# Measured charges and a shared read port in the clock that orders a two-network kernel

## The chip, the cores and the metric

The kernel runs on one core of a Trainium2 chip. The metric is the device time of one execution in microseconds (us). The core's engines are TensorE (PE in the rows; PEld are its weight loads), VectorE (DVE), ScalarE (ACT), GpSimd (POOL), and SyncE (SP), which issues most of the transfers. TensorE's clock has two levels here, 2.4 and 1.2 GHz; the profile gives the granted share of 2.4 GHz for any stretch.

## What is computed

Two networks run one after the other on 512 tokens of width 1024, in float32, and share nothing but the kernel. Cut to what matters:

```
# first network, one layer
h = h + 0.5 * rms_norm(swiglu(rms_norm(h), w_gate, w_up, w_down))
u = rms_norm(h) @ w_in                       # q, k, v of two mixers
o_a = stick_breaking_attention(...)          # 8 heads of 64
o_b = chunk_band_attention(...)              # 8 heads of 64, 9 chunks of 64
h = h + rms_norm(concat(rms_norm(o_a), rms_norm(o_b)) @ w_out)
h = h + 0.5 * rms_norm(swiglu(rms_norm(h), ...))
h = h + rms_norm((p @ w_proj) * sigmoid(h @ w_ple_gate))

# second network, four layers, x = x + mixer(rms_norm(x)), then a last norm
conv:  (b * causal_conv(c * v)) * silu(z) @ w_out
fox:   softmax(q k^T + forget decay) v, 8 heads of 128
gdn:   gated delta net, 8 heads of 128, chunks of 64: a triangular solve for each chunk
swa:   rotary, windowed attention of 128 with sinks, 16 heads of 64
```

## The kernel before

Activations stand transposed: a tile holds 128 channels by 512 tokens, and the residual stream is eight such tiles, h0 to h7. Weights come from HBM as 128x512 chunks into four staging tiles (`wst`), and each chunk is split in two: ScalarE copies the high part (fp32r), VectorE subtracts it for the low part. A product is three fp32r matmuls (high by high, low by high, high by low), summed in a PSUM bank.

An rms norm needs three steps that leave TensorE and come back. Squares of the eight h tiles are added into one tile (ScalarE squares, VectorE or GpSimd adds); TensorE sums the columns with matmuls of one column (`stats`, line 820, in the rows `ps<-cst,t ... 128x1`); a chain of small operations takes the reciprocal root, on VectorE with `soon`, else on GpSimd (`rsqrt`, line 786, thirteen operations); and TensorE spreads it over the rows by transposes (`rows`, line 842, in the rows `ps<-cst,b 128x128` of line 687). Only then can results be scaled. So that TensorE does not stand still, matmuls of the next weights are put between these steps: each layer's first products run on the unscaled h.

Nothing here is ordered by hand. The program is written out instruction by instruction, and a clock kept while that is done (lines 255 to 590) decides what comes next. `free[...]` holds for each engine the time at which it comes free, each tile the time of its last write or read. Calls on VectorE, ScalarE, GpSimd and SyncE go through `Eng` (line 358), which charges them by formulas and leaves them pending as `Op`; `next_op` (line 336) takes the one that can start first (among those within 20 ns the one of the best rank) and `trace` writes it out. TensorE's matmuls are charged by `mm` (line 669) and `transpose` (line 684) and written out at once by `product`. Side tasks are generators (the norms, the heads of the mixers); between the matmuls of a weight product `poll` (line 566) runs a step of a side task when the clock says that what it needs is there. A charge that is changed therefore moves instructions on every engine, and each engine then works its list strictly in order.

Every recorded VectorE, ScalarE and GpSimd operation has line 391 in the rows, every matmul line 682 and every transpose line 687, since helpers write them out.

Of the kernel before, what the change touches and what calls it, by code (L numbers as in the profile page):

```python
# [201 lines left out]
def chain_kernel(ctx, tc, xT, pT, wall, params, consts, chbias, pos, out):  # L202
# [82 lines left out]
    table = [None]  # L285

    class Op:


        def __init__(self, key, run, outs, ins, cost, prio=0, func=None, more=0):  # L290
            self.key, self.run, self.outs, self.ins, self.cost, self.more = key, run, outs, ins, cost, more
            self.prio, self.func = prio, func
            self.deps, self.next = set(), []
            for x, w in [(x, True) for x in outs] + [(x, False) for x in ins]:
                for o in conflicts(x, w):
                    if o not in self.deps:
                        self.deps.add(o)
                        o.next.append(self)
            for x, w in [(x, True) for x in outs] + [(x, False) for x in ins]:
                live.setdefault(name(x), []).append((self, parts(x)[0], w))  # L300
            pending[key].append(self)
# [9 lines left out]

        def start(self):
            return max([free[self.key]] + [there(x, self.key) for x in self.ins] + [unused(x, self.key) for x in self.outs])

        def trace(self):
# [7 lines left out]
            self.run()  # L323
            free[self.key] = t
            pending[self.key].remove(self)
            for x in self.outs + self.ins:
# [9 lines left out]
    def next_op():  # L336

        best, when = None, NEVER
        for ops in pending.values():
            can = [(o.start(), o) for o in ops if not o.deps]  # L340
            if can:
                t0 = min(c[0] for c in can)
                t, o = min((c for c in can if c[0] <= t0 + 20), key=lambda c: c[1].rank())
                if t < when:
                    best, when = o, t
        return best, when

# [10 lines left out]
    class Eng:  # L358
# [6 lines left out]
        def __getattr__(self, op):  # L365
            f = getattr(self.eng, op)

            def call(*a, **kw):
# [19 lines left out]
                else:  # L388
                    a0, a1 = (258, 3.34) if ptr else self.POOL.get(op, (147, 2.1))
                    cost = a0 + a1 * n  # L390
                Op(self.key, lambda: f(*a, **kw), outs, ins, cost, self.prio, func, more)  # L391

# [265 lines left out]
    def product(ps, ins, ns):  # L658
# [8 lines left out]
        touch(ps, t + ns, "PE", True)  # L667

    def mm(ps, lhsT, rhs, start=True, stop=True, tile=None, **kw):
        ps, lhsT, rhs = raw(ps), raw(lhsT), raw(rhs)  # L670
        n = max(parts(rhs)[1], 64)
        if tile is not None:
            ns = tile
        elif rhs.dtype == F32:
            ns = 4 * n / 2.4 + 2.5
        elif rhs.dtype == F32R:
            ns = (n if n >= 256 else 4 * n) / 2.4 + 2.5
        else:
            ns = n / 2.4
        thin[0] = max(0.0, thin[0] + (ns if tile is not None else -0.5 * ns))  # L680
# [3 lines left out]
    def transpose(ps, src, idn):  # L684
        ps, src, idn = raw(ps), raw(src), raw(idn)
        product(ps, (src, idn), 107.0)
        PE.transpose(ps, src, idn)  # L687
# [110 lines left out]
    class Norm:  # L798
# [21 lines left out]
        def stats(self, cols, soon=False):  # L820
# [3 lines left out]
            for j in range(c0 // P, c1 // P):  # L824
                mm(pc[:, j : j + 1], self.acc[:, j * P : j * P + P], meanc[:, self.mcol : self.mcol + 1], start=j == c0 // P,
                   skip_group_check=True, tile=187)
            self.left -= c1 - c0
# [272 lines left out]
    def soft_heads(heads, span, done, own, causal=False, ready=lambda: True):  # L1100
# [46 lines left out]
        def weigh(qt):  # L1147
            k0, n = span(qt)
            for j in range(n // P):
                for i, (rows, qk, bias, values, sinks) in enumerate(heads):  # L1150
                    mm(po[rows, qt * P : qt * P + P], values(k0 // P + j), ptb[qt, i][:, j * P : j * P + P],
                       start=j == 0, stop=j == n // P - 1, skip_group_check=True, tile=134 if len(heads) > 1 else None)
            for i in range(len(heads)):
# [23 lines left out]
    def mixing(S1):  # L1177
# [45 lines left out]
        def sb_pair(p):  # L1223
# [93 lines left out]
            for kt in range(4):  # L1317
                for e in range(2):
                    hd = 2 * p + e
                    mm(po[rows[e], kt * P :], va[kt][:, hd * 64 : hd * 64 + 64], at_(a[place[kt, e][0]], kt, e), start=kt == 0, stop=kt == 3, skip_group_check=True,  # L1320
                       tile=0.95 * (S - kt * P))
            a.clear()
# [284 lines left out]
    def gdn_layer(S1):  # L1607
# [18 lines left out]
        def gates(t):  # L1626
            yield t[0:64]
            pt = PS("bat")
            for c in range(4):
                mm(pt[:, c * 16 : c * 16 + 16], t[0:64, c * P : c * P + P], con("ident32")[0:64, 0:16], tile=187)  # L1630
            del t
# [59 lines left out]
        def head(hd):  # L1691
# [88 lines left out]
            def mm32(ps, lhsT, rhs):  # L1780
                for c in range(4):
                    for g in range(4):
                        gs, cs = slice(32 * g, 32 * g + 32), slice(32 * c, 32 * c + 32)
                        mm(ps[gs, cs], lhsT[gs, cs], rhs[gs, cs], tile=34)

# [26 lines left out]
            for c in range(4):  # L1812
                cs = slice(32 * c, 32 * c + 32)
                for a, b in zip(lo, hi):
                    mm(p5[b, cs], nL[a, c * P + b.start : c * P + b.stop], Tm[a, cs], tile=34)
            for i, b in enumerate(hi):
# [7 lines left out]
            for c in range(4):  # L1824
                cs = slice(32 * c, 32 * c + 32)
                mm(p7[hi[0], cs], U[hi[0], cs], M5[hi[0], cs], tile=34)
                for a, b in zip(lo, hi):
                    mm(p6[a, cs], M5[b, cs], U[b, cs], tile=34)
            V.tensor_copy(blocks(T64[:, 0:256])[hi[0], :, 0:32], blocks(p7[:, 0:P])[hi[0]])
# [5 lines left out]
            for c in range(4):  # L1835
                cs = slice(64 * c, 64 * c + 64)
                mm(p8[64:P, cs], nL[0:64, c * P + 64 : c * P + P], T64[0:64, cs], tile=50)
            M6 = T64
# [301 lines left out]
```

## Time and profile before

| | |
|---|---|
| median of three runs | 2174.5 us (2173.39 to 2176.55) |
| profiled execution | 2176.79 us |
| its span, first to last instruction | 2175.1 us |
| mean granted TensorE clock | 0.990 |
| TensorE busy | 2116.3 us, 97% |
| VectorE busy | 1324.4 us, 61% |
| ScalarE busy | 999.2 us, 46% |
| GpSimd busy | 299.5 us, 14% |

The span is what the profile's rows cover; the 1.7 us between it and the execution's time lie outside of any instruction. A timeline row gives the start, the duration from the first to the last instruction of the row, engine, line, operation, output and inputs by the program's names, shape and count; in brackets stands the idle time of the engine ahead of the row and what ended it. A matmul's duration contains its way through the array, so the pace is read from a row of many.

### The profile page before, as it was taken

Reading aid. Unit: us, or ns where it says so; the run is one execution under the profiler, and the core shown is the slowest. Engines: PE = TensorE matmul, PEld = TensorE weight load, DVE = VectorE, ACT = ScalarE, POOL = GpSimd, SP = SyncE. Lnnn points to the kernel's source line nnn. Section 1 sums busy time; section 2 is a strip of 40 time slices with the busy share of each in tenths; the row PEclk is TensorE's granted clock in tenths of the full one; section 3 lists DMA queues with packets and bytes.
Section 4 is the critical chain, followed back from the end, with each engine's and each line's share of the span. In section 5 each row is a group of like instructions: output and inputs, shape, how many; then the busy total and the mean of one; then the engine's idle time right before and its main releaser. Section 6 shows DMA issues by size and latency. Waiting matters only on the chain.

```text
span 2175.1 us, 35809 instructions
## 1 busy us (share of the span) xinstructions
PE 2116.3 (97%) x13583; PEld 1778.1 (82%) x13583; DVE 1324.4 (61%) x2783; ACT 999.2 (46%) x2187; POOL 299.5 (14%) x600
## 2 busy tenths in 40 slices
PE   8999999999999999999999999999998999999998
PEld 7888889988779888889988887888877877778777
DVE  5433455787867442455785554266568677665896
ACT  5332333676855332333642234344446554533764
POOL 0000001311113000000120012000015242221320
PEclk9999999999999999999999999999999999999999
DMA  5232241222221332232223333312222222222221
GB/s 170 97 97 93 96 139 56 69 70 81 64 88 52 105 112 83 97 115 71 92 73 97 97 97 115 116 59 68 69 85 70 60 55 59 61 83 86 85 83 59
DMA packets 105404, 186.11 MB, mean 86 GB/s; under 512 B 12392, under 2 KB 18952, under 8 KB 105232
## 3 DMA queue, kind: packets, MB, share of 16 engines
q1 hardware_dynamic: 103920, 179.62, 26.6%
q0 software_dynamic: 1312, 4.21, 0.6%
q8 instruction: 106, 1.74, 0.3%
q14 instruction: 66, 0.54, 0.1%
HBM read 179.03 MB, written 2.13 MB: 83 GB/s over the span
## 4 chain that ended last, share of the span: by engine, by line
PE 82%; DVE 11%; POOL 3%; ACT 2%; issue 2%; DMA 1%; SPq 0%; DVEq 0%; POOLq 0%; ACTq 0%
PE ps L682 80%; DVE t L391 9%; ACT t L391 2%; PE ps L687 2%; POOL b L391 2%; DVE h L391 1%; POOL t L391 1%; DVE b L391 0%; DMA wst<-in_wall_dram 0%; DMA h<-in_xT_dram 0%; ACT L391 0%; DVE pad L391 0%; SPq L391 0%; POOL h L391 0%; DVE a L391 0%
## 5 line engine op out<-in xcount | busy, mean ns | idle before, releaser
L682 PE MATMUL ps<-t,t 128*128 128x512 f32 (+4 forms) x10648 | 2035.2, 353 | 22.1 <-ACT t L391 11.3
L682 PEld LDWEIGHTS ps<-t,t 128*128 128x128 f32 (+2 forms) x10648 | 1678.2, 186 | 320.7 <-issue 24.4
L391 DVE TENSOR_TENSOR t<-wst,t 128x512 fp32r<-128x512 f32 (+1 forms) x646 | 448.4, 719 | 252.6 <-ACT t L391 250.7
L391 ACT ACTIVATE t<-t 128x512 f32<-128x512 f32 (+4 forms) x470 | 260.3, 569 | 608.8 <-DVE t L391 602.0
L391 ACT ACTIVATE t<-wst 128x512 fp32r<-128x512 f32 (+1 forms) x646 | 380.8, 621 | 98.3 <-DMA wst<-in_wall_dram 94.9
L391 DVE TENSOR_TENSOR t<-ps,t 128x512 f32<-128x512 f32 (+2 forms) x247 | 156.1, 638 | 297.7 <-PE ps L682 296.0
L391 DVE TENSOR_TENSOR t<-t,t 128x512 fp32r<-128x512 f32 (+6 forms) x387 | 238.4, 631 | 66.7 <-ACT t L391 60.8
L391 ACT ACTIVATE t<-ps 128x512 f32<-128x512 f32 (+5 forms) x357 | 140.5, 418 | 239.0 <-PE ps L682 155.5
L391 POOL TENSOR_TENSOR t<-t,t 128x512 f32<-128x512 f32 (+1 forms) x99 | 120.0, 1213 | 542.1 <-ACT t L391 463.7
L391 POOL TENSOR_TENSOR h<-h,t 128x256 f32<-128x256 f32 x40 | 34.7, 874 | 795.5 <-DVE t L391 793.9
L391 ACT ACTIVATE t<-t,a 128x257 f32<-128x257 f32 (+5 forms) x128 | 66.2, 518 | 49.4 <-DVE a L391 46.8
L391 ACT ACTIVATE t<-h,prm 128x256 fp32r<-128x256 f32 (+1 forms) x80 | 46.4, 588 | 83.4 <-DVE h L391 69.8
L391 DVE SCALAR_TENSOR_TENSOR t<-h,prm,t 128x256 fp32r<-128x256 f32 (+1 forms) x80 | 64.2, 815 | 9.0 <-ACT t L391 9.0
L391 DVE SCALAR_TENSOR_TENSOR t<-pad,prm,t 128x512 f32<-128x512 f32 (+1 forms) x92 | 68.7, 755 | 0.8
L687 PE MATMUL ps<-cst,t 128*128 128x128 f32 x400 | 63.1, 279 | 2.5 <-DVE t L391 1.7
L391 ACT ACT_TABLE_LOAD x48 | 61.6, 1283 | 5.7 <-DVE a L391 4.1
L687 PEld LDWEIGHTS ps<-cst,t 128*128 128x128 f32 x400 | 48.6, 143 | 14.8 <-DVE t L391 2.5
L391 ACT ACTIVATE t<-h 128x256 f32<-128x256 f32 (+2 forms) x112 | 49.6, 466 | 22.6 <-DVE h L391 20.3
L391 POOL TENSOR_SCALAR b<-b 128x4 f32<-128x4 f32 (+3 forms) x84 | 26.1, 310 | 206.8 <-DVE b L391 201.7
L682 PEld LDWEIGHTS ps<-t 32*32 32x32 f32 (+1 forms) x2304 | 33.1, 109 | 24.3 <-DVE t L391 10.4
L391 DVE TENSOR_SCALAR t<-t,a 128x256 f32<-128x256 f32 (+3 forms) x128 | 49.2, 394 | 2.3
L391 POOL TENSOR_SCALAR_AFFINE_SELECT t<-t 128x256 f32<-128x256 f32 (+2 forms) x48 | 27.3, 571 | 168.0 <-DVE t L391 117.1
(93 smaller groups left out, 693.1 us busy)
## 6 DMA issues: line engine op xcount, KB each, us to landing
wst<-in_wall_dram SPq DMA_DIRECT2D x644, 256.0 KB, 2.7
t<-t SPq DMA_DIRECT2D x40, 64.0 KB, 2.0
h<-in_xT_dram SPq DMA_DIRECT2D x8, 256.0 KB, 5.3
t<-in_chbias_dram POOLq DMA_DIRECT2D x8, 256.0 KB, 3.7
t<-cdr POOLq DMA_DIRECT2D x8, 256.0 KB, 6.4
t<-gdr SPq DMA_DIRECT2D x32, 64.0 KB, 3.7
out_dram<-t SPq DMA_DIRECT2D x16, 128.0 KB, 1.8
cst<-in_consts_dram SPq DMA_DIRECT2D x1, 626.0 KB, 6.3
```

What stands on the lines that cost most here:

```text
L391: Op(self.key, lambda: f(*a, **kw), outs, ins, cost, self.prio, func, more)
L682: PE.matmul(ps, lhsT, rhs, start=start, stop=stop, **kw)
L687: PE.transpose(ps, src, idn)
```

## The change

The clock gets other numbers. First, a read port: `port[0]` is the time at which it comes free. GpSimd's operations, and VectorE's that read no PSUM and have two wide inputs or are of the kinds in `FAST` (`tensor_scalar`, `tensor_copy`, `memset`), are `shared`: they start no earlier than the port is free and hold it to their end. Among engines `next_op` compares the start with the port and, where it is equal, the start without it. Second, operations on 32 to 127 partitions are charged 115 ns more. Third, TensorE's charges: fp32r (n + 32) / 2.4 ns instead of n / 2.4 + 2.5, other formulas for fp32 and bf16, 95 ns for each change of the tile size, 110 instead of 107 ns for a transpose, and other constants for the small products.

The program gets no other instruction, but for two more table loads on ScalarE (51 instead of 49) that come from the order. Helper lines shift: 391 becomes 404, 682 becomes 708, 687 becomes 713.

```diff
+    port = [0.0]
     class Op:
-        def __init__(self, key, run, outs, ins, cost, prio=0, func=None, more=0):
+        def __init__(self, key, run, outs, ins, cost, prio=0, func=None, more=0, shared=False):
...
-        def start(self):
-            return max([free[self.key]] + [there(x, self.key) for x in self.ins] + [unused(x, self.key) for x in self.outs])
+        def start(self, port_too=True):
+            t = max([free[self.key]] + [there(x, self.key) for x in self.ins] + [unused(x, self.key) for x in self.outs])
+            return max(t, port[0]) if self.shared and port_too else t
...
             free[self.key] = t
+            if self.shared:
+                port[0] = t
...
-                if t < when:
+                t = t, o.start(False)
+                if t < when:
...
+                if op != "dma_start" and any(32 <= x.ap[0][1] < P for x in outs + ins):
+                    cost += 115
+                wide = [x for x in ins if parts(x)[1] > 1]
+                shared = self.key == "POOL" or self.key == "DVE" and not ps and (len(wide) > 1 or op in self.FAST)
...
+    mode = [(P, P)]
+    CHANGE = 95.0
+
+    def changed(rows, cols):
+        new = tuple(next(x for x in (32, 64, P) if n <= x) for n in (rows, cols))
+        if new == mode[0]:
+            return 0.0
+        mode[0] = new
+        return CHANGE
...
     def mm(ps, lhsT, rhs, start=True, stop=True, tile=None, **kw):
...
-        n = max(parts(rhs)[1], 64)
+        n = parts(rhs)[1]
...
-            ns = 4 * n / 2.4 + 2.5
+            ns = 2 * max(110.0, (2 * n + 8) / 2.4)
...
-            ns = (n if n >= 256 else 4 * n) / 2.4 + 2.5
+            ns = ((n if n >= 256 else 4 * n) + 32) / 2.4
...
-            ns = n / 2.4
+            ns = max(n, P) / 2.4 + 2.5
+        ns += changed(rhs.ap[0][1], parts(lhsT)[1])
...
-        product(ps, (src, idn), 107.0)
+        product(ps, (src, idn), 110.0 + changed(P, P))
...
-                   skip_group_check=True, tile=187)
+                   skip_group_check=True, tile=220)
...
-                       start=j == 0, stop=j == n // P - 1, skip_group_check=True, tile=134 if len(heads) > 1 else None)
+                       start=j == 0, stop=j == n // P - 1, skip_group_check=True, tile=110 if len(heads) > 1 else None)
...
-                       tile=0.95 * (S - kt * P))
+                       tile=0.84 * (S - kt * P))
...
-                        mm(ps[gs, cs], lhsT[gs, cs], rhs[gs, cs], tile=34)
+                        mm(ps[gs, cs], lhsT[gs, cs], rhs[gs, cs], tile=25)
```

What moves is shown at three places. In the names, `ps` is a PSUM bank, `wst` a staged weight chunk, `h_257` the tile h7, `t` a wide and `b` a small working tile, `cst` the constants.

VectorE, end of gdn, where h7 gets its last sum and swa's norm begins. Before:

```order
L391 TENSOR_TENSOR t_27_18286<-wst_247,t_29_18285 128x512
L391 CAST t_24_18308<-t_36_18307 128x512
L391 TENSOR_SCALAR c_228<-prm 128x16
L391 TENSOR_TENSOR t_29_18312<-wst_248,t_27_18311 128x512
L391 TENSOR_SCALAR t_24_18308<-t_24_18308,prm 128x512
L391 TENSOR_SCALAR t_28_18309<-t_24_18308 128x512
L391 COPY t_24_18310<-t_28_18309 128x512
L391 TENSOR_TENSOR h_257<-ps_238,h_257 128x512
```

And after:

```order
L404 TENSOR_TENSOR h_257<-ps_235,h_257 128x512
L404 CAST t_23_18305<-t_28_18304 128x512
L404 TENSOR_SCALAR c_228<-prm 128x16
L404 TENSOR_TENSOR t_31_18281<-wst_247,t_29_18280 128x512
L404 SCALAR_TENSOR_TENSOR t_33_18300<-h_257,prm,t_29_18299 128x512
L404 TENSOR_SCALAR t_23_18305<-t_23_18305,prm 128x512
L404 TENSOR_TENSOR t_36_18309<-wst_248,t_37_18308 128x512
L404 TENSOR_SCALAR t_26_18306<-t_23_18305 128x512
```

The add into h7 has moved ahead of seven instructions, to directly behind the split of h6; weight subtractions and the steps of swa's angles follow it.

TensorE, end of fox, where gdn's norm sums the columns (the row with 128x1) among matmuls of gdn's first weights. Before:

```order
L682 MATMUL ps_236<-t_28_13891,t_34_13948 128x512
L682 MATMUL ps_241<-t_26_13890,t_34_13948 128x512
L682 MATMUL ps_241<-t_26_13890,t_28_13949 128x512
L682 MATMUL ps_241<-t_28_13891,t_34_13948 128x512
L682 MATMUL ps_240<-cst,t_20_13889 128x1 x4
L682 MATMUL ps_239<-t_26_13890,t_34_13948 128x512
```

And after:

```order
L708 MATMUL ps_239<-t_28_13890,t_18_13947 128x512
L708 MATMUL ps_239<-t_28_13890,t_33_13948 128x512
L708 MATMUL ps_239<-t_19_13891,t_18_13947 128x512
L708 MATMUL ps_241<-t_18_13893,t_36_13972 128x512
L708 MATMUL ps_241<-t_18_13893,t_23_13973 128x512
L708 MATMUL ps_241<-t_14_13894,t_36_13972 128x512
L708 MATMUL ps_234<-cst,t_35_13889 128x1 x4
L708 MATMUL ps_238<-t_18_13893,t_36_13972 128x512
```

The sums stand nine matmuls later: the rest of this weight chunk and the first three of the next now come ahead of them. At the end of gdn the same sums stand six matmuls later and their transposes 33.

VectorE, end of the first network, where the second half of the tokens is scaled by the rows of the norm (eight operations that read one bank, `ps_239` before and `ps_241` after) and split for the convolution. Before, the last of them:

```order
L391 TENSOR_TENSOR h_255<-h_255,t_28_10132 128x256
L391 SCALAR_TENSOR_TENSOR t_18_9909<-h_254,prm,t_23_9903 128x256
L391 TENSOR_TENSOR t_24_10258<-wst_247,t_25_10257 128x512
L391 SCALAR_TENSOR_TENSOR t_15_10134<-t_16_9785,b_198,ps_239 128x256
L391 SCALAR_TENSOR_TENSOR t_24_9918<-h_255,prm,t_14_9907 128x256
L391 SCALAR_TENSOR_TENSOR t_20_10136<-t_17_9817,b_198,ps_239 128x256
```

And after, all eight:

```order
L404 SCALAR_TENSOR_TENSOR t_15_10148<-t_13_9515,b_198,ps_241 128x256
L404 SCALAR_TENSOR_TENSOR t_24_10149<-t_19_9517,b_198,ps_241 128x256
L404 TENSOR_TENSOR h_250<-h_250,t_15_10148 128x256
L404 SCALAR_TENSOR_TENSOR t_22_10151<-t_21_9519,b_198,ps_241 128x256
L404 SCALAR_TENSOR_TENSOR t_23_10153<-t_24_9521,b_198,ps_241 128x256
L404 SCALAR_TENSOR_TENSOR t_23_10155<-t_16_9717,b_198,ps_241 128x256
L404 SCALAR_TENSOR_TENSOR t_21_10157<-t_14_9756,b_198,ps_241 128x256
L404 SCALAR_TENSOR_TENSOR t_19_10159<-t_25_9787,b_198,ps_241 128x256
L404 SCALAR_TENSOR_TENSOR t_19_10161<-t_18_9817,b_198,ps_241 128x256
```

Before, additions into h, splits of h and weight subtractions stand between the eight; after, one addition does, and the rest follows.

## Rows read from the trace of the kernel before

**Rows 1.** The page: busy time of an engine; chain that ended last, by engine.
```profile
PE 2116.3 (97%) x13583; PEld 1778.1 (82%) x13583; DVE 1324.4 (61%) x2783; ACT 999.2 (46%) x2187; POOL 299.5 (14%) x600
...
PE 82%; DVE 11%; POOL 3%; ACT 2%; issue 2%; DMA 1%; SPq 0%; DVEq 0%; POOLq 0%; ACTq 0%
```
**Rows 2.** TensorE's waits, whole span: total us, times, longest.
```profile
PE ps L682 <- DVE t L391: 22.9, 25, 2.7
...
PE ps L682 <- POOL t L391: 6.0, 3, 2.9
...
PE ps L687 <- POOL b L391: 3.9, 2, 2.7
```
**Rows 3.** Timeline between fox and gdn: column sums, matmuls behind, matmuls at full clock.
```profile
1587.48 1.05 PE L682 MATMUL ps<-cst,t 128*128 128x1 f32 x8 [2.07 <-POOL t L391]
...
1588.39 6.65 PE L682 MATMUL ps<-t,t 128*128 128x512 f32 x21
...
1595.23 7.09 PE L682 MATMUL ps<-t,t 128*128 128x512 f32 x30
```
**Rows 4.** Stretches: us, busy time of the engines, granted clock (PEclk), DMA share, GB/s.
```profile
1090.20:1093.60 3.40, 3.40 (x18) 3.40 (x17) 2.34 (x7) 3.15 (x7) 2.84 (x4) 0.51 0.25 77
...
1108.90:1112.30 3.40, 3.40 (x28) 3.40 (x29) 3.40 (x8) 2.81 (x5) 2.42 (x4) 1.00 0.16 59
...
1953.70:1957.10 3.40, 3.40 (x9) 2.63 (x9) 3.37 (x8) 0.00 (x0) 1.14 (x2) 0.50 0.24 82
```
**Rows 5.** Timeline between gdn and swa.
```profile
1946.20 0.68 DVE L391 TENSOR_TENSOR t<-wst,t 128x512 fp32r<-128x512 f32 x1
...
1949.14 0.68 DVE L391 TENSOR_TENSOR h<-ps,h 128x512 f32<-128x512 f32 x1
...
1952.56 1.05 PE L682 MATMUL ps<-cst,t 128*128 128x1 f32 x8 [2.89 <-POOL t L391]
...
1953.47 6.63 PE L682 MATMUL ps<-t,t 128*128 128x512 f32 x21
...
1962.84 0.65 PE L687 MATMUL ps<-cst,b 128*128 128x128 f32 x4 [2.74 <-POOL b L391]
...
1963.25 8.94 PE L682 MATMUL ps<-t,t 128*128 128x512 f32 x31
```
**Rows 6.** Stretch from the first network's last norm into the convolution (columns as in rows 4).
```profile
1085.00:1120.00 35.00, 30.07 (x236) 29.46 (x236) 30.90 (x73) 20.76 (x45) 16.49 (x19) 0.95 0.20 61
```
**Rows 7.** Timeline of that stretch.
```profile
1087.09 0.95 DVE L391 TENSOR_TENSOR h<-h,t 128x256 f32<-128x256 f32 x1
...
1089.21 0.61 PE L682 MATMUL ps<-cst,t 128*128 128x1 f32 x4 [1.84 <-DVE t L391]
...
1089.68 5.32 PE L682 MATMUL ps<-t,t 128*128 128x256 f32 x30
...
1095.77 3.47 PE L682 MATMUL ps<-t,t 128*128 128x256 f32 x27
...
1108.88 3.37 PE L682 MATMUL ps<-t,t 128*128 128x256 f32 x26 [2.15 <-DVE t L391]
```
**Rows 8.** Timeline at the end of the mixing.
```profile
610.61 0.65 PE L687 MATMUL ps<-cst,b 128*128 128x128 f32 x4 [1.13 <-POOL b L391]
```
**Rows 9.** TensorE's waits from 1650 to 1925; timeline there; 32x32 matmuls by form.
```profile
PE ps L682 <- DVE t L391: 9.7, 10, 2.7
...
1658.92 0.45 PE L682 MATMUL ps<-t 32*32 32x32 f32 x32 [2.63 <-DVE t L391]
...
1677.73 0.96 PE L682 MATMUL ps<-t,t 128*128 128x512 f32 x3
...
1678.62 0.45 PE L682 MATMUL ps<-t 32*32 32x32 f32 x32
...
1683.38 0.45 PE L682 MATMUL ps<-t 32*32 32x32 f32 x32 [2.73 <-DVE t L391]
...
L682 PE MATMUL ps<-t 32*32 32x32 f32 x2240 | 32.6, 194 | 7.2 <-DVE t L391 6.9 <-ACT t L391 0.2
```

More of the change, by code (lines that the diff above doesn't have):

```diff
@@ L285, in chain_kernel @@
     table = [None]
+    port = [0.0]
     class Op:
-        def __init__(self, key, run, outs, ins, cost, prio=0, func=None, more=0):
+        def __init__(self, key, run, outs, ins, cost, prio=0, func=None, more=0, shared=False):
             self.key, self.run, self.outs, self.ins, self.cost, self.more = key, run, outs, ins, cost, more
+            self.shared = shared
             self.prio, self.func = prio, func
@@ L336, in next_op @@
     def next_op():
-        best, when = None, NEVER
+        best, when = None, (NEVER, NEVER)
         for ops in pending.values():
@@ L343, in next_op @@
                 t, o = min((c for c in can if c[0] <= t0 + 20), key=lambda c: c[1].rank())
+                t = t, o.start(False)
                 if t < when:
                     best, when = o, t
-        return best, when
+        return best, when[0]
     def advance(t):
@@ L390, in call @@
                     cost = a0 + a1 * n
-                Op(self.key, lambda: f(*a, **kw), outs, ins, cost, self.prio, func, more)
+                if op != "dma_start" and any(32 <= x.ap[0][1] < P for x in outs + ins):
+                    cost += 115
+                wide = [x for x in ins if parts(x)[1] > 1]
+                shared = self.key == "POOL" or self.key == "DVE" and not ps and (len(wide) > 1 or op in self.FAST)
+                Op(self.key, lambda: f(*a, **kw), outs, ins, cost, self.prio, func, more, shared and op != "dma_start")
             return call
@@ L1629, in gates @@
             for c in range(4):
-                mm(pt[:, c * 16 : c * 16 + 16], t[0:64, c * P : c * P + P], con("ident32")[0:64, 0:16], tile=187)
+                mm(pt[:, c * 16 : c * 16 + 16], t[0:64, c * P : c * P + P], con("ident32")[0:64, 0:16], tile=220)
             del t
@@ L1814, in head @@
                 for a, b in zip(lo, hi):
-                    mm(p5[b, cs], nL[a, c * P + b.start : c * P + b.stop], Tm[a, cs], tile=34)
+                    mm(p5[b, cs], nL[a, c * P + b.start : c * P + b.stop], Tm[a, cs], tile=40)
             for i, b in enumerate(hi):
@@ L1825, in head @@
                 cs = slice(32 * c, 32 * c + 32)
-                mm(p7[hi[0], cs], U[hi[0], cs], M5[hi[0], cs], tile=34)
+                mm(p7[hi[0], cs], U[hi[0], cs], M5[hi[0], cs], tile=40)
                 for a, b in zip(lo, hi):
-                    mm(p6[a, cs], M5[b, cs], U[b, cs], tile=34)
+                    mm(p6[a, cs], M5[b, cs], U[b, cs], tile=40)
             V.tensor_copy(blocks(T64[:, 0:256])[hi[0], :, 0:32], blocks(p7[:, 0:P])[hi[0]])
@@ L1836, in head @@
                 cs = slice(64 * c, 64 * c + 64)
-                mm(p8[64:P, cs], nL[0:64, c * P + 64 : c * P + P], T64[0:64, cs], tile=50)
+                mm(p8[64:P, cs], nL[0:64, c * P + 64 : c * P + P], T64[0:64, cs], tile=124)
             M6 = T64
```

## Prediction

> **What bounds the kernel now.** I read four views in turn. The page's busy times and its chain say which engine sets the end: TensorE is busy 97% of the span and the chain runs on it for 82% [rows 1]. No work is added or taken away by this change, so only what TensorE loses can move the time. The wait table then says where TensorE stands still and for whom: 22.9 us in 25 waits for a VectorE tile, 6.0 us in three for a GpSimd sum, and 3.9 us in two for GpSimd's reciprocal roots [rows 2]. The last two rows are five waits that hold 9.9 us, three of them at two norms between layers, so the next view is the timeline there [rows 3, 5]. The last view is the granted clock in the stretch behind such a wait: 0.50 or 0.51 of 2.4 GHz, the lower level of 1.2 GHz, in stretches that begin about 1 us after TensorE resumed [rows 4] (behind 1587.48 and 1962.84 it is 0.50 as behind 1952.56). A long wait is thus paid twice, once as idle time and once as slow matmuls.
>
> The price of the slow part: at the higher level 30 matmuls of 128x512 take 7.09 us, 0.236 each, while 21 of them behind the wait of 2.07 us took 6.65 us [rows 3]. 21 x 0.236 = 4.96, so 1.7 us were lost to the clock.
>
> **The change part by part.** The edits alter only the clock that orders instructions while the program is written out: a read port that VectorE and GpSimd take in turn, other charges for TensorE, 115 ns more for operations on some of the partitions. The same instructions stay on each engine. What they do is read from the two orders, and its price from the trace.
>
> *Fox to gdn, near 1587 us.* TensorE waits 2.07 us at the column sums of squares for the GpSimd add behind the last residual add, into h7 [rows 3]. In the new order nine more weight matmuls stand ahead of those sums: 9 x 0.236 = 2.1 us of cover, as much as the wait. h7's add also goes ahead of two weight subtractions and a cast on VectorE, so the sum comes earlier too. The transposes of the root come nine matmuls later and did not wait before. The wait goes (2.07), the slow stretch behind it with it (1.7): **-3.8 us**. The bound on the other side is 0, if the clock falls and the wait comes back at the transposes. What would be late next is the ScalarE copy of the transposed roots, for which no row here waits.
>
> *Gdn to swa, 1945 to 1975 us.* The largest pair. VectorE starts h7's add at 1949.14. Ahead of it, from 1946.20, it works off seven instructions [rows 5]: two weight subtractions and the first steps of swa's sines, which nothing reads for ten microseconds. TensorE waits 2.89 us for what hangs on h7 (ScalarE square, GpSimd add), then 2.74 us at the transposes at 1962.84 for the chain of thirteen small GpSimd operations [rows 5]. In the new order h7's add stands ahead of all seven: it starts 1949.14 - 1946.20 = 2.9 us earlier, as long as the first wait. Six more matmuls (1.4 us) stand ahead of the column sums besides. The transposes come 33 places later: 48 matmuls then stand between sums and transposes, 48 x 0.236 = 11.3 us, against the 1962.84 - 1952.56 = 10.3 us that the way between took. Both waits go (5.6), and both slow stretches: 6.63 - 4.96 = 1.7 for 21 matmuls, 8.94 - 31 x 0.236 = 1.6 for 31 [rows 5]. Sum **-8.9 us**, bounds -8.9 and -4.5 (one wait with its stretch stays).
>
> The sine and cosine operations and the weight subtractions pushed behind h7 have their readers at 1958 us and later, so I cost their delay at nothing; without that cover it would be their 2.9 us.
>
> *End of the first block into the convolution, 1085 to 1120 us.* VectorE does everything here, 30.90 of 35 us [rows 6]. TensorE waits 1.84 us at 1089.21 and 2.15 us at 1108.88, and its 30 matmuls of 128x256 behind the first took 5.32 us, against 3.47 / 27 x 30 = 3.86 [rows 7]. The new order takes an add into h (0.95 us) and a split of h from ahead of the sum and puts one scaled product, as long as the split, there: 0.95 us earlier [rows 7]. It also writes all eight scaled products of the second half in a row, where before other work stands between them; they all read one PSUM bank, and the matmul at 1108.88 waits for that bank [rows 7]. At most 0.9 + 1.5 + 2.15 = 4.5 us are won. But the splits of h stand behind now, and the stretch has only 35 - 30.90 = 4.1 us of VectorE idle time. I take **-3.5 us**, bounds -4.5 and 0.
>
> *End of the mixing, 605 to 613 us.* The column sums of the first norm are written 14 small matmuls later, its transposes four later, and the VectorE copy that frees the attention output four places later. The way from sums to transposes already waits 1.13 us [rows 8]. With ten places of cover fewer (14 less 4, some 0.07 us each) and the chain later by a VectorE operation or so: **+1.2 us**, bounds -0.6 (last scores two microseconds earlier, ScalarE full anyway) and +2.
>
> *Gdn's heads, 1650 to 1925 us.* The order is shuffled throughout. TensorE waits 9.7 us here in ten waits for VectorE [rows 9], and hardly for others. One of the two long ones (2.63 us at 1658.92) gets 3.4 us more work ahead of its consumer and goes; the other (2.73 us at 1683.38) gets none [rows 9]. I laid both orders over the trace's durations: of 228 groups of matmuls that wait for another engine 98 get less cover by over 0.2 us, 75 more; 34 are short of it before, 54 after. With 9.7 / 34 = 0.29 us for one that is short, 20 more cost 5.7 us. Some are short only by what a queue held up before, so I take half, 2.9. In the two orders tile-size changes on TensorE go from 283 to 295, charged 95 ns in the change, bounded from above by the step into the 32x32 group at 1678.62 (1678.62 - 1677.73 less three matmuls of 0.236 leaves 0.18) [rows 9]: 12 x 0.095 = 1.1, at most 2.2, at least 0. 2.9 + 1.1 - 2.6 = **+1.4 us**, bounds -5.4 (both long waits go, no new one) and +7.9 (5.7 and 2.2, no wait goes).
>
> *Smaller sites* (first norm, the two norms before and behind the mixing, swa): waits of 0.4 to 1.3 us that the new order covers in part and opens elsewhere; two more table loads on ScalarE, which has the time (46% busy). **-1.0 us**, bounds -2 and +2.
>
> Sum: -3.8 - 8.9 - 3.5 + 1.2 + 1.4 - 1.0 = -14.6 us, from the profiled execution's 2176.8 us to 2162.2. That execution is 2.3 us above the median of the runs, so the forecast is **2160 us**.
>
> **A rule against one of the terms.** In the sum the slow stretches count 1.7 + 1.7 + 1.6 + 1.5 = 6.5 us, as if each hung on the wait ahead of it. The rows are not that strict: the wait of 1.84 us was followed by the lower clock, that of 2.15 us at 1108.88 was not (1.00) [rows 4, 7]. The Trainium skill, TensorE: Matmul & The Clock Gate, Part 1: The HAM clock gate, says that the activity window runs freely, so how many matmuls run slow varies between runs of one kernel. By that rule the 6.5 us are a matter of phase and may come back elsewhere, and the sum would be -8.1; by the rows, where every slow stretch between matmuls that I named stands behind a wait of 1.84 us or more, they go with the waits. I keep the rows and make the other a rival.
>
> **The rivals.** (a) *The clock falls all the same.* The idle time goes, but shorter waits at the same norms still bring the lower clock: -14.6 + 6.5 = -8.1, so 2166 us. For it: the wait at 1089.21 shrinks only by half. Against it: at the two other norms the waits go whole. (b) *Gdn takes it back, and the kernel is slower.* The clock now lets a GpSimd operation and a two-input VectorE operation exclude each other, so the short VectorE steps between 32x32 products are written in other places among convolution operations of 0.7 us. The rows hold 2240 matmuls of 32x32, 70 groups of 32 [rows 9]; the eight shorter VectorE waits took (9.7 - 2.63 - 2.73) / 8 = 0.54 us each. If 27 more groups wait so, the gain is gone; with 40, +21.6 - 14.6 = +7: 2182 us. Against it: half the shuffled groups gain cover. (c) *The places move but not the starts*: matmuls put ahead of the sums wait themselves, for weights not yet split, since the splits were pushed behind h7. Then the waits change their names and the time stays within 0.2% of 2174.5. Against it: those weights were split ten microseconds ahead.
>
> **How the numbers follow.** A measurement of this kernel tells about 0.2% (4.3 us) from no change, so faster is below 2170.2 us. Forecast 0.62 (2150 to 2169); (a) 0.12; (b) 0.11; (c) and gdn taking back just the gain 0.09; better than all terms, below 2149, 0.06. Faster is 0.62 + 0.12 + 0.06 = 0.80, same 0.09, slower 0.11. The range leaves out the best 0.06, (b) and the upper part of (c): 2149 to 2174. The lower end is the sum with its good bounds in gdn, the convolution, the smaller sites and the mixing (-14.6 - 6.8 - 1.0 - 1.0 - 1.8 = -25.2), the upper the bad gdn bound with rival (a) (-8.1 + 6.5 = -1.6).
>
> **What would show it.** Right, if the wait table has at most one GpSimd wait in the two norms near 1587 and 1952 and the granted clock there stays 1.00; if the matmuls near 1108 run on without the 2.15 us; if gdn's wait total stays below 14 us. Wrong, if the two norms still show waits of 2 us at their transposes, if gdn's table shows 20 or more waits for VectorE, or if 1085 to 1120 takes as long as now with VectorE above 33 us busy.

## The result and the profile after

The changed kernel takes 2143.5 us in the median (2142.89 to 2144.42) beside 2175.3 us for the kernel before (2173.39 to 2176.55): a ratio of 0.9855, interval 0.9838 to 0.9872. It is 31.7 us faster, where 15 were forecast, and below the range of 2149 to 2174. The direction and most of the places were right; half of the gain came from places that the sum had at plus 1.4 and minus 1.0 us.

The profiled execution has a span of 2141.6 us (2175.1 before) and a mean granted clock of 0.993 (0.990). TensorE's waits over the whole span, answering [rows 2] (us in total, times, longest):

```profile
PE ps L708 <- ACT t L404: 14.7, 8, 5.4
PE ps L708 <- DVE t L404: 9.0, 11, 2.2
PE ps L713 <- DVE b L404: 3.8, 2, 2.5
...
PE ps L708 <- POOL b L404: 0.6, 1, 0.6
PE ps L708 <- POOL t L404: 0.2, 1, 0.2
```

Waits for a VectorE tile went from 22.9 us in 25 to 9.0 in 11. The GpSimd sums, 6.0 us before, hold 0.2, and the row for the roots at the transposes (3.9 us) is gone.

The two norms, answering [rows 3] and [rows 5]; timeline of the kernel after, first fox to gdn, then gdn to swa:

```profile
1577.95 1.05 PE L708 MATMUL ps<-cst,t 128*128 128x1 f32 x8 [0.19 <-POOL t L404]
1578.86 5.01 PE L708 MATMUL ps<-t,t 128*128 128x512 f32 x21
...
1918.10 1.77 DVE L404 SCALAR_TENSOR_TENSOR t<-h,prm,t 128x512 fp32r<-128x512 f32 x1
...
1921.06 0.68 DVE L404 TENSOR_TENSOR h<-ps,h 128x512 f32<-128x512 f32 x1
...
1925.82 0.95 PE L708 MATMUL ps<-cst,t 128*128 128x1 f32 x8
...
1926.63 11.19 PE L708 MATMUL ps<-t,t 128*128 128x512 f32 x48
...
1937.66 0.60 PE L713 MATMUL ps<-cst,b 128*128 128x128 f32 x4
```

The wait of 2.07 us is 0.19, and the 21 matmuls behind it take 5.01 us instead of 6.65. At the second norm neither the sums nor the transposes have a bracket left, and the 48 matmuls between them run at 0.233 us each. The granted clock there, answering [rows 4] (us, busy times, clock in the third column from the end):

```profile
1578.00:1582.00 4.00, 4.00 (x22) 3.48 (x23) 0.77 (x2) 0.00 (x0) 2.04 (x9) 1.00 0.46 148
1925.00:1929.00 4.00, 4.00 (x23) 3.44 (x22) 3.90 (x10) 0.83 (x2) 1.47 (x3) 1.00 0.49 138
```

Where the rest came from is seen by the starts of the same matmul in both traces. The table gives what each stretch of the program gained (minus) or lost, in us, for the change and for two of the experiments; stretches are named by the times of the kernel before. In e4 the mixing has its matmuls in another order, so there the sum of its two rows (+3.1) is firmer than either.

| stretch | forecast | change | e4, port alone | e3, no port |
|---|---|---|---|---|
| 372-416, norm behind the first FFN | in "smaller" | -5.1 | -3.8 | +3.0 |
| 416-574, mixing | in "smaller" | -1.3 | +3.5 | +0.1 |
| 574-625, end of the mixing | +1.2 | +2.3 | -0.4 | +4.1 |
| 625-698, norm behind the mixing | in "smaller" | +0.1 | -2.1 | +3.4 |
| 1084-1120, into the convolution | -3.5 | -4.7 | -3.2 | +1.8 |
| 1578-1600, fox to gdn | -3.8 | -3.5 | -3.9 | +0.5 |
| 1600-1925, gdn | +1.4 | -11.8 | -16.5 | +0.7 |
| 1945-1975, gdn to swa | -8.9 | -9.3 | -9.3 | -0.6 |
| 2000-2150, swa | in "smaller" | +0.6 | +8.0 | +1.2 |
| whole span | -14.6 | -33.5 | -28.3 | +16.9 |

In gdn TensorE now waits for almost nothing. Waits of the kernel after between 1600 and 1930, answering [rows 9], where the first row had 9.7 us:

```profile
PE ps L708 <- DVE t L404: 1.6, 4, 0.4
PE ps L713 <- ACT t L404: 0.9, 1, 0.9
PE ps L708 <- POOL b L404: 0.6, 1, 0.6
```

The norm behind the first FFN was one of the "smaller sites". Two pairs of rows, first of the kernel before, then of the kernel after:

```profile
375.13 0.61 PE L682 MATMUL ps<-cst,t 128*128 128x1 f32 x4 [1.07 <-POOL t L391]
...
378.42 0.61 PE L682 MATMUL ps<-cst,t 128*128 128x1 f32 x4 [1.15 <-DVE t L391]
```

```profile
375.24 0.50 PE L708 MATMUL ps<-cst,t 128*128 128x1 f32 x4
...
376.40 0.50 PE L708 MATMUL ps<-cst,t 128*128 128x1 f32 x4
```

Both sums wait before, neither does after, and between 364 and 400 us the wait table of the kernel after is empty (before, up to 405 us, it holds 2.9 us for VectorE and 1.1 for GpSimd).

The new order also opens something. At the norm behind the mixing the transposes wait 2.51 us for VectorE's chain (1.21 before, at 673.08), and a slow stretch follows that the kernel before does not have; timeline and stretch of the kernel after:

```profile
675.60 0.43 PE L713 MATMUL ps<-cst,b 128*128 128x128 f32 x2 [2.51 <-DVE b L404]
...
676.70:679.90 3.20, 3.20 (x17) 3.20 (x16) 3.20 (x9) 3.17 (x6) 0.40 (x1) 0.50 0.24 81
```

### The profile page after: what moved, and what is told of

Read it like the earlier page. It is cut to its first block, busy times and chain, and to the rows that moved or that the text cites. A ratio compares the mean times of both kernels' runs of the same rounds, so it can differ in the third digit from the quotient of the medians.

```text
span 2141.6 us, 35794 instructions
## 1 busy us (share of the span) xinstructions
PE 2102.8 (98%) x13583; PEld 1771.5 (83%) x13583; DVE 1304.2 (61%) x2783; ACT 1004.1 (47%) x2189; POOL 291.1 (14%) x600
## 4 chain that ended last, share of the span: by engine, by line
PE 91%; DVE 4%; ACT 3%; issue 1%; DMA 1%; POOL 0%; SPq 0%; DVEq 0%; ACTq 0%; POOLq 0%
PE ps L708 89%; DVE t L404 3%; ACT t L404 3%; PE ps L713 2%; ACT L404 0%; DMA wst<-in_wall_dram 0%; POOL t L404 0%; DMA h<-in_xT_dram 0%; SPq L404 0%; DVE b L404 0%; DVE h L404 0%; POOL b L404 0%; DVE pad L404 0%; DVE a L404 0%; POOL h L404 0%
## 5 line engine op out<-in xcount | busy, mean ns | idle before, releaser
L708 PEld LDWEIGHTS ps<-t,t 128*128 128x128 f32 (+1 forms) x10648 | 1674.8, 186 | 314.9 <-issue 22.0
L404 DVE SCALAR_TENSOR_TENSOR t<-h,prm,t 128x256 fp32r<-128x256 f32 (+1 forms) x80 | 56.0, 725 | 8.4 <-ACT t L404 8.2
L404 DVE CUSTOM_DVE_ANT_0 t<-ps,t 128x128 f32<-128x128 f32 (+3 forms) x64 | 30.4, 487 | 26.2 <-PE ps L708 25.3
```

The costliest lines, as they stand in the source:

```text
L708: PE.matmul(ps, lhsT, rhs, start=start, stop=stop, **kw)
```

## Experiments

The change has three factors: the port, TensorE's charges, and 115 ns on some partitions. The first four runs separate them. Theory 1 says that the port is what moves the work to the right places, theory 2 that TensorE's charges empty gdn of waits.

**e1, TensorE's charges alone** (against the changed kernel):

```diff
-                    cost += 115
+                    cost += 0
-                shared = self.key == "POOL" or self.key == "DVE" and not ps and (len(wide) > 1 or op in self.FAST)
+                shared = False
```

> Of the change only TensorE's charges are kept; no read port, no 115 ns. Theory 1 (the port moves the residual adds and the GpSimd sums to where the chip does them, and that is what ends the waits): in this order the column sums stand 3 matmuls earlier than before at the end of gdn and where they were at the end of fox, so the waits of 2 to 3 us with their slow stretches stay at both, and gdn keeps some 8 of its 10 us of waits: 2165 to 2185 us. Theory 2 (the measured charges of the small matmuls are what empties gdn of waits): gdn's waits fall below 4 us, and with the waits at the two norms left the time is 2155 to 2165.

Measured: 2195.1 us, ratio to before 1.0089 (1.0074 to 1.0104).

**e2, without TensorE's charges**: `mm`, `transpose` and the constants as before, port and 115 ns kept. (One constant differs from both kernels: four small products of each gdn head, `p9`, are charged 50 ns instead of 124, here and in e4. What that does was not measured.)

> The change without TensorE's charges: read port and 115 ns. Theory 1: the column sums stand 3 matmuls later than before at the end of fox and their transposes 15 later, the transposes at the end of gdn 30 later, h7's add moves up on VectorE: both pairs of waits go for the most part, and gdn loses most of its waits: 2143 to 2155 us. Theory 2: gdn keeps 7 us or more of waits and one of its slow stretches: 2157 to 2168.

Measured: 2159.7 us, ratio 0.9925 (0.991 to 0.994).

**e3, without the port** (`shared = False`, the rest of the change kept).

> The change without the read port: TensorE's charges and 115 ns on some partitions. Theory 1: like e1 at the two norms and in gdn, 2165 to 2185 us. Theory 2: gdn below 4 us of waits, 2155 to 2165. Only the end of the mixing differs from e1 in where the column sums stand (150 matmuls of small size later), worth 3 us at most.

Measured: 2196.8 us, ratio 1.0098 (1.0081 to 1.0115).

**e4, the port alone** (as e2, and `cost += 20` in place of 115).

> The read port alone, with 20 ns in place of 115 on some partitions and TensorE's old charges. Theory 1: within 4 us of e2, so 2143 to 2158 us. Theory 2: gdn keeps 7 us or more of waits, 2157 to 2168.

Measured: 2149.8 us, ratio 0.9879 (0.9864 to 0.9893).

Theory 2 falls: without the port the charges make the kernel slower than before by 20 us, and with the port alone it is faster by 26. By its time alone e2 would speak for theory 2, but what that theory says of gdn fails there too: between 1600 and 1930 the wait table of e2 is empty, and gdn gains 17.2 us with TensorE's old charges. Waits between 1600 and 1930 of each kernel's own time, of e3 and then of e4:

```profile
PE ps L708 <- DVE t L404: 9.5, 10, 3.9
PE ps L708 <- POOL t L404: 2.6, 1, 2.6
PE ps L713 <- DVE t L404: 0.7, 1, 0.7
```

```profile
PE ps L695 <- DVE t L404: 0.9, 3, 0.4
```

e1 and e3 came out worse than either theory said, and e2 some 5 us above theory 1. The 10 us between e2 and e4 lie in the mixing and at its end, where e2 loses 14.1 us between 416 and 640 and e4 3.1: in e2's order the sums of the second norm stand 48 matmuls later than before, and TensorE waits 2.17 us at them and 3.92 at their transposes. Beside the port the charges win back part of what the port alone costs: in the mixing and at its end e4 loses 3.1 us and in swa 8.0, the whole change 1.0 and 0.6.

**e5, busy waits.** The kernel before, its order untouched, with idle transposes that fill three of the waits:

```diff
             pc = PS("nrc")
+            busy(pc[:, P : 2 * P], self.fill[0])    # 18 at fox to gdn, 26 at gdn to swa
...
             ps = PS("nrm")
+            busy(ps[:, :P], self.fill[1])           # 24 at gdn to swa
```

> The kernel before, in its own order, with transposes that nothing reads put on TensorE ahead of the column sums at the two norms (18 at the end of fox, 26 at the end of gdn) and ahead of the transposes at the end of gdn (24): they fill the waits of 2.07, 2.89 and 2.74 us and shorten nothing. Theory A (the lower clock hangs on the idle time ahead of it): the granted clock stays at 1.00 behind the three places and the slow matmuls go, 1.7 + 1.7 + 1.6 = 5.0 us: 2169 to 2172 us against some 2175.5. Theory B (the lower clock is a matter of phase): it falls there all the same or elsewhere, and the time stays within 2 us of the kernel before.

Measured: 2175.0 us, ratio 0.9995 (0.9986 to 1.0005). Timeline of e5:

```profile
1589.26 5.05 PE L682 MATMUL ps<-t,t 128*128 128x512 f32 x21
...
1682.84 0.65 PE L682 MATMUL ps<-t 32*32 32x32 f32 x32 [2.89 <-DVE t L391]
...
1954.26 5.02 PE L682 MATMUL ps<-t,t 128*128 128x512 f32 x21
...
1963.63 0.65 PE L687 MATMUL ps<-cst,b 128*128 128x128 f32 x4 [1.74 <-POOL b L391]
```

Theory A is right on the clock at the three places: with the waits filled the same 21 matmuls take 5.05 and 5.02 us instead of 6.65 and 6.63. Its price fails: 5 us of slow matmuls went there, and 0.8 us of time. The 1.6 us gained at 1954 are waited for again at 1963, since the GpSimd chain between sums and transposes sets that time: filler and rest of the wait together are longer than the old one. That slow stretch cost nothing, because the wait behind it ends by GpSimd.

More was lost as theory B has it, to the lower clock elsewhere, in instructions that e5 leaves as they were. First the kernel before, then e5 (columns of the stretch as in [rows 4]):

```profile
630.80:634.00 3.20, 3.20 (x16) 2.63 (x15) 3.20 (x7) 1.64 (x4) 0.00 (x0) 1.00 0.04 5
...
1686.96 2.15 PE L682 MATMUL ps<-t,t 128*128 128x512 f32 x16
```

```profile
630.80:634.00 3.20, 3.20 (x9) 2.48 (x8) 3.20 (x7) 0.86 (x2) 0.00 (x0) 0.50 0.18 61
...
1686.85 2.83 PE L682 MATMUL ps<-t,t 128*128 128x512 f32 x16
```

Ahead of the stretch at 630 both traces have the same wait of 1.56 us for ScalarE; it was followed by the lower clock in e5 and not in the kernel before. In gdn the wait at 1682.84 is 0.16 us longer than before and the clock stays low longer behind it; 1.3 of the 1.6 us won at fox to gdn are gone by 1700. So the lower clock came behind idle times, but the same idle time brought it in one execution and not in another.

**e6, zeros elsewhere.** The kernel before, with the zero fills of the heads run by ScalarE in GpSimd's place of the order:

```diff
-            G.memset(UU, 0.0)
-            G.memset(T64[0:64, 0:256], 0.0)
+            zero(UU, UU)                               # nc.scalar.activation(..., scale=0.0)
+            zero(T64[0:64, 0:256], UU[0:64, 0:256])
```

> The kernel before, in its own order, with the two zero fills of each gdn head done by ScalarE (a copy with scale 0) in the place where GpSimd had them. Theory C (the wait of 2.73 us at 1683 came from VectorE copies held up by GpSimd memsets at the same port): the four copies at 1678 take about 1.1 us together instead of 2.79, the wait falls below 1.3 us and the slow stretch behind it goes: 2171 to 2174 us. Theory D (the copies are late by their place in the order): the wait stays above 2 us and the time within 1.5 us of before.

Measured: 2172.8 us, ratio 0.9983 (0.9973 to 0.9992). The site in the kernel before, then in e6:

```profile
1678.12 2.28 POOL L391 MEMSET t<- 128x512 f32 x6
1678.16 2.79 DVE L391 COPY t<-t 32x128 f32<-32x128 f32 x4
```

```profile
1678.49 0.90 DVE L391 COPY t<-t 32x128 f32<-32x128 f32 x4
...
1681.83 0.45 PE L686 MATMUL ps<-t 32*32 32x32 f32 x32 [0.83 <-DVE t L391]
...
1683.00:1686.00 3.00, 3.00 (x63) 2.00 (x67) 2.92 (x10) 2.03 (x5) 0.00 (x0) 1.00 0.28 73
```

Theory C holds. The four copies take 0.90 us when GpSimd does not fill beside them, the wait falls from 2.73 to 0.83 us, and the clock behind it stays at 1.00: 3.0 us by one collision. The Trainium skill, SBUF — State Buffer, Who interferes with whom, says that copies can contend with GpSimd for a shared pair of ports; these rows agree.

**e7, the port for two-input operations alone:**

```diff
-... and not ps and (len(wide) > 1 or op in self.FAST)
+... and not ps and len(wide) > 1
```

> The whole change, but on VectorE only operations with two wide inputs take the port; copies and tensor_scalars are free of it in the clock. The two norms have their column sums and transposes where the whole change has them, so their waits are gone in any case. If the copies' share of the port is what cleared gdn (theory C), gdn keeps 3 us or more of waits and the time is 2147 to 2153 us. If two-input operations are enough, 2141 to 2146.

Measured: 2140.4 us, ratio 0.9836 (0.9821 to 0.985). Two-input operations are enough (the time is even 0.6 us below the range for that); gdn keeps its gain of 11 us. So the collision of e6 is one of the ways in which gdn lost time, but it takes no port charge on the copies to end it.

**e8, the old charges while gdn is written out** (the change elsewhere; transposes and one small product, `p8`, keep the new ones).

> The whole change, but while gdn is written out TensorE is charged as before. The port alone won 16.5 us between the start and the end of gdn, the whole change 11.8. If the old charges suit gdn better, 2137 to 2141 us. If e4's gain there hung on what came ahead of gdn, 2141 to 2148.

Measured: 2137.9 us, ratio 0.9825 (0.9811 to 0.984): gdn gains 16 us, as with the port alone.

**e9, e7 and e8 together.**

> e7 and e8 together: two-input operations alone take the port, and TensorE has its old charges while gdn is written out. e7 won 5.4 us over the whole change at the end of the mixing and lost 1.6 at the end of gdn, e8 won 4.2 in gdn. If these add up: 2133 to 2137 us. If gdn's order depends on what stands ahead of it: 2137 to 2143.

Measured: 2134.8 us, ratio 0.9813 (0.9798 to 0.9828). Faster than both kernels, and in total the two gains add up: 3.1 and 5.6 us over the whole change alone, 8.7 together. By place they do not: gdn gains 13.8 us here and 16 in e8.

**e10, a slower clock in place of turns:**

```diff
+                if shared and op != "dma_start":
+                    cost *= 1.2
-                Op(..., more, shared and op != "dma_start")
+                Op(..., more)
```

> The whole change, but nobody takes turns: the operations that would share the port are charged 20% more instead. Theory E (the exclusion matters: VectorE's clock must fall back where GpSimd runs beside it and nowhere else): no better than without the port, 2175 to 2200 us; the column sums stand where the kernel before has them. Theory F (any slower VectorE clock does it): 2143 to 2160 us.

Measured: 2183.3 us, ratio 1.0035 (1.0021 to 1.0048). That lies in the range of theory E, but not all of theory E holds: e10 is 13.6 us better than e3, which has no port at all. The even slowing brings a part of the gain, 4.9 us in gdn (the change 11.8), 4.0 at gdn to swa (9.3) and 1.1 at fox to gdn (3.5). And 11.2 of what it loses lie between 416 and 640, where the sums of the second norm stand 48 matmuls later, as they do in e2, which has the port and loses 14.1 us there. So 20% on every such operation does not replace the taking of turns; another size was not tried.

**e11, the port for copies and other single-input kinds alone** (`len(wide) < 2 and op in self.FAST`).

> The whole change, but on VectorE only the single-input kinds (copies, tensor_scalars, fills from SBUF) take the port. Theory E with two-input operations as the ones that matter (after e7): like e3, 2188 to 2200 us. If the copies beside GpSimd's fills matter as much: gdn loses its waits and the time is below 2175.

Measured: 2193.7 us, ratio 1.0086 (1.0071 to 1.0101): like no port at all.

**e12, h7 first.** The kernel before with one operation written out earlier:

```diff
             V.tensor_tensor(h[m], ps, h[m], ALU.add)
+            if m == 7 and layer == 3:
+                list(pending["DVE"])[-1].trace()
```

> The kernel before with one thing moved: at the end of gdn the add into h7 is written out as soon as its product is, ahead of six of the seven instructions that stood before it (2.3 us); TensorE's sums and transposes come three matmuls earlier by that. If the place of the add is the term: the sums start 2.3 us earlier, the transposes too, and 2 to 4 us are won: 2171.5 to 2174. If the matmuls put ahead of sums and transposes are what counts, and VectorE's place nothing: within 1 us of the kernel before.

Measured: 2174.8 us, ratio 0.9996 (0.9986 to 1.0006), not told apart from before. Timeline of e12:

```profile
1946.80 0.68 DVE L391 TENSOR_TENSOR h<-ps,h 128x512 f32<-128x512 f32 x1
...
1950.34 1.05 PE L682 MATMUL ps<-cst,t 128*128 128x1 f32 x8 [1.36 <-POOL t L391]
...
1960.28 0.95 PE L687 MATMUL ps<-cst,b 128*128 128x128 f32 x4 [3.96 <-POOL b L391]
```

The add starts 2.3 us earlier, the sums 2.2, the transposes 2.6, as expected, and the same matmuls behind this place start 1.9 us earlier. But the transposes still wait, 3.96 us now. By these two traces VectorE's place alone is worth some 2 of the 9.3 us, too little for the runs to show. That the rest needs the matmuls which the change puts ahead of the transposes fits the rows, but no run moves those alone.

## Why the prediction was right and wrong

The sum failed at two of its terms, gdn and the smaller sites; the other four were right in sign, and three of them in size. The signs named for being right all came true (0.19 us of GpSimd wait at the two norms and a granted clock of 1.00 there, 0.69 us instead of 2.15 at the convolution, 3.1 us of waits in gdn), but they set no bound to a gain in gdn. By the sum named for it the upper end of the range is 2172.9, not 2174 us; nothing hangs on that.

**What bounds the kernel**: right. No work changed. Of the 33.5 us of span 20.0 are TensorE's idle time (58.8 us before, 38.8 after) and 13.5 its busy time. Outside the mixing and the very end six stretches of 3.4 us at half the clock stand before and one after, some 8.5 us less; the other 5 us of busy time are not assigned.

**Fox to gdn (-3.8, measured -3.5) and gdn to swa (-8.9, measured -9.3)**: right in mechanism and size. The rows show each step: the sums' waits, the transposes' wait, the slow stretches. One reason was off. I added the two slow stretches of the second norm to its two waits, as if each could be won alone. e5 shows that the first is won only together with the transposes' wait; the sum held because the change ends both.

**Into the convolution (-3.5, measured -4.7)**: right, a little small. I capped it by VectorE's idle time of 4.1 us. The matmul behind the freed bank waits 0.69 us instead of 2.15:

```profile
1096.27 7.94 PE L708 MATMUL ps<-t,t 128*128 128x256 f32 x64 [0.69 <-DVE t L404]
```

The cap was wrong in kind: VectorE's work itself got shorter. The same 72 VectorE instructions that start between 1085 and 1120 us before take 36.0 us there and 33.3 in the kernel after.

**End of the mixing (+1.2, measured +2.3)**: right in sign, not in mechanism, and the place where the change costs most. The wait at the first norm's transposes, 1.13 us, was to grow; it is gone. The sums of the second norm now stand ahead of these transposes, and they wait:

```profile
604.20 1.22 PE L708 MATMUL ps<-cst,t 128*128 128x1 f32 x8 [2.18 <-DVE t L404]
...
605.38 1.12 PE L713 MATMUL ps<-cst,b 128*128 128x128 f32 x4
```

**Gdn (+1.4, measured -11.8)**: wrong, and the larger part of the miss. The good bound of -5.4 counted the two long waits alone. In fact all waits of gdn together fell from 10.6 to 3.1 us, and both slow stretches went, some 1.7 us each: 10.9 of the 11.8. The two stretches in the kernel before, then the same places in the kernel after (columns as in [rows 4]):

```profile
1660.20:1663.60 3.40, 3.40 (x15) 3.00 (x14) 3.40 (x9) 2.50 (x14) 1.52 (x2) 0.50 0.55 152
...
1684.10:1687.50 3.40, 3.40 (x39) 2.34 (x38) 2.69 (x8) 0.78 (x2) 0.00 (x0) 0.50 0.23 74
```

```profile
1643.00:1647.00 4.00, 3.58 (x76) 2.46 (x75) 3.56 (x9) 1.54 (x3) 1.20 (x4) 1.00 0.38 132
1666.00:1670.00 4.00, 4.00 (x78) 2.73 (x70) 3.84 (x12) 2.74 (x9) 0.69 (x2) 1.00 0.04 11
```

Three steps of the term failed.
- The count of covers. I held each round trip's duration as it was in the trace of before, queues included, against the matmuls that cover it in the new order, and found 34 short before and 54 after. With the instructions of the two programs matched one by one, 231 of gdn's round trips can be compared in the traces: 130 have less time between product and consumer, but in 89 of these the way through the other engines is shorter too. Consumers that started within 0.35 us of their input, that is, had waited for it or nearly, fell from 22 to 12. The port reorders VectorE's list in the same stroke, so a duration that is mostly queue can't be carried over (that it was mostly queue is the reading that fits these counts, not a run of its own).
- The wait at 1683, which I left standing because its cover did not grow. In the kernel before it came for the most part from one collision of four copies with GpSimd's fills: without it 0.83 of 2.73 us are left (e6). What ended it in the changed order is not shown; e7 shows that it did not take the copies' share of the port.
- The slow stretches behind the two long waits, which I priced at the norms and forgot here. e6 won 3.0 us where its wait shrank by 1.9; the rest fits the slow stretch, which is gone too.

**Smaller sites (-1.0, measured some -6)**: wrong in size. The norm behind the first FFN alone gave 5.1 us. I had the small sites' waits covered in part and others opened; here all 4.0 us of waits went and none came. What fills VectorE there shrinks too: the same 86 VectorE instructions, those that start between 365 and 418 us before, take 45.1 us before and 41.6 after, which fits two-input operations that stand beside a GpSimd operation less often.

**The rule on the clock**: the sum stood by the rows, and in the kernel after the slow stretches are gone with the waits at all the places it named (1.00 there). Rival (a) did not happen at these norms. But the rows were not the whole of it: e5 shows the clock to stay up where the idle time is filled, and to fall elsewhere behind an idle time that had not brought it down before, and the change has one slow stretch of its own at 676.7. That all of the stretches in the sum went and only one came is in part luck.

**Rival (b)**, that gdn takes the gain back, did not happen with the port. Without a port for two-input operations gdn as a whole does lose, 9.7 us in e1, 0.7 in e3 and 3.3 in e11; whether by the mechanism of (b) is not shown. **Rival (c)** did not happen.

**The cause, as far as it is shown.** The clock must know that GpSimd and two-input VectorE operations exclude each other. Without that the charges, with or without single-input operations in the port, lose 18 to 21 us (e1, e3, e11); with the port alone 26 us are won (e4), and the whole change keeps all of its gain when only two-input operations take it (e7). The port for two-input operations with nothing else changed was not run, and a clock slowed evenly by 20% does not replace it (e10). Rows of the kernel before show what the old clock missed: the split of an h tile with no GpSimd operation beside it, then GpSimd's adds at the end of gdn and the split of h6 beside them:

```profile
1585.54 0.75 DVE L391 SCALAR_TENSOR_TENSOR t<-h,prm,t 128x512 fp32r<-128x512 f32 x1 [0.85 <-ACT t L391]
...
1940.68 5.04 POOL L391 TENSOR_TENSOR t<-t,t 128x512 f32<-128x512 f32 x3 [1.48 <-ACT t L391]
...
1944.50 1.77 DVE L391 SCALAR_TENSOR_TENSOR t<-h,prm,t 128x512 fp32r<-128x512 f32 x1
```

The old clock charges 0.66 us for a split (68 + 1.04 x 512 + 61 ns), the chip takes 0.75 us alone and 1.77 here; in the kernel after a split of this kind still takes 1.77 (the row at 1918.10), but there the clock counts the wait for GpSimd. With VectorE's clock ahead of the chip by such steps, the program fills time on VectorE that isn't there, with weight splits and sines, and the add that TensorE waits for stands behind them. That the lag of the clock leads to this at each place is argued from the order at three of them, not shown for all.

Open: why TensorE's measured charges, which beside the port win back part of the losses in the mixing and in swa, cost 17 us and more without it, and why gdn does better with the old ones (e8). No run takes the charges apart, and 115 ns on some partitions cost 10 us between e4 and e2 without a reason shown.

## What to carry to other kernels

When an order comes from a clock, model first what two engines exclude each other from; in this kernel more accurate single charges made the order worse while that was missing. Price a reorder by the path's own operations, not by durations that contain the old order's queues. And before a slow or idle stretch is counted as gain, look at the next wait behind it: if that ends by another engine, as at gdn to swa here, nothing is won until that one is moved too.

## What the runs showed of the hardware

- Six GpSimd fills of 2.28 us together stretched four VectorE copies from 0.90 to 2.79 us.
- A two-input VectorE operation of 128x512 took 1.77 us beside GpSimd's adds and 0.75 us alone.
- TensorE's clock stayed at the higher level through waits that were filled with fp32 transposes (e5), and the same 21 matmuls took 5.05 us instead of 6.65.
- The same instructions behind the same wait of 1.56 us ran at 1.00 of the clock in the kernel before and at 0.50 in e5 (630.8 to 634.0).
- In a GpSimd chain of thirteen small operations most take 0.2 us each where VectorE stands still (1580 us) and 0.37 to 0.65 us beside VectorE's operations, the two-input ones above all (1928 to 1935 us). In the kernel before the chain at 1957 us shows the same. From the kernel after:

```profile
1580.79 0.20 POOL L404 TENSOR_TENSOR b<-b,b 128x4 f32<-128x4 f32 x1
...
1930.59 0.65 POOL L404 TENSOR_TENSOR b<-b,b 128x4 f32<-128x4 f32 x1
```
